# Gelu of a sum: one ScalarE pass over z itself, six equal transfers, and most adds on VectorE

## The chip, the core and the metric

The kernel runs on one core of a Trainium2 chip. The metric is device time in microseconds (us), the median over runs of the same program. One further execution is recorded by the hardware profiler, and its trace is what the views below are taken from.

The engines that appear are VectorE (DVE), ScalarE (ACT), GpSimd (POOL) and SyncE (SP), whose queue issues all transfers. The transfers themselves are carried out by 16 DMA engines.

## The reference

```
x, y: float32 [1024, 4096], random normal
z = x + y
out = 0.5 * z * (1 + tanh(sqrt(2 / pi) * (z + 0.044715 * z ** 3)))
```

This is the tanh form of gelu applied to a sum. Nothing is reduced and nothing is reused: 33.55 MB are read, 16.78 MB are written.

## The kernel before

The 1024 x 4096 tensors are viewed as 128 partitions of 32768 floats each, so every partition holds 128 KB of x, of y and of the result. One tile `z` of that size lies in SBUF. x is loaded straight into it, y is added to it in place, and the results are written over it and stored from it. y itself passes through two buffers of 8192 floats (32 KB) for each partition, used in turn.

All transfers are issued on SP, in one fixed order: the first quarter of y, the first half of x, the second quarter of y, the second half of x, the third and fourth quarters of y (lines 126 and 133), and then three stores of 16384, 10240 and 6144 floats for each partition (line 137). One row of a transfer is what one partition receives or gives, so rows of x are 64 KB, rows of y are 32 KB, and those of the stores 64, 40 and 24 KB. The first two loads are issued ahead of everything else (`begin_early`). The third and fourth loads of y wait until the adds have read the buffer that they overwrite. The first store waits, besides its data, for the first closing step of chunk 8 (`FIRST`).

The work is cut into 16 chunks of 2048 floats for each partition. A chunk goes through four steps:

- `add` (line 150): z = x + y in place, for chunks 0, 2, 4, 6, 8 and 12 on VectorE, for the other ten on GpSimd.
- `mag` (line 155): ScalarE writes |z| to a PSUM tile `w`; there are two such tiles.
- `gelu` (line 158): ScalarE applies its gelu-tanh function to -|z| in place in PSUM.
- `end` (line 167): VectorE writes max(z, 0) + w over z, which is gelu(z), since gelu(z) = max(z, 0) + gelu(-|z|).

The order on each engine is written out by hand: lists for SP, POOL, ACT and DVE are merged by a loop that takes a step when everything in `needs` is done, inside a manual schedule. The four lists and the table of needs are what fixes who waits for whom. At the end, the last wait for the last store is put behind all other closing work (`wait_late`).

Of the kernel before, what the change touches and what calls it, by code (L numbers as in the profile page):

```python
# [8 lines left out]
def begin_early(nc, count):  # L9


    head, body = (b.instructions for b in nc.main_func.blocks[:2])
    SP = mybir.EngineType.SP
    moved = [i for i in body if i.engine == SP and isinstance(i, mybir.InstDMACopy)][:count]
    assert not any(i.sync_info and i.sync_info.on_wait for i in moved)
    assert all(i.regs_accessed() == ((), ()) for i in moved)
    at = next(k for k, i in enumerate(head) if i.engine == SP)
    for k, i in enumerate(moved):
        body.remove(i)
        head.insert(at + k, i)  # L20


def wait_late(nc):

    body, end = (b.instructions for b in nc.main_func.blocks[1:3])
    last = [i for i in body if isinstance(i, mybir.InstDMACopy)][-1]
    (sem,) = [u.id for u in last.sync_info.on_update]
    all_done = end[0]  # L30
    reset = next(i for i in end if isinstance(i, mybir.InstDrain) and i.is_reset_sema)
    at = end.index(reset)
    clear = end[at + 1]
    first, stop = reset.reset_range_start, reset.reset_range_stop
    assert all_done.engine == mybir.EngineType.SP and reset.engine == mybir.EngineType.Pool
    assert isinstance(clear, mybir.InstISA) and clear.engine == mybir.EngineType.Pool
    waits = all_done.sync_info.on_wait
    (its,) = [w for w in waits if w.id == sem]

    end[0] = mybir.InstDrain(  # L40
        name=all_done.name, engine=all_done.engine, debug=all_done.debug, is_reset_sema=False,
        sync_info=mybir.SyncInfo(on_wait=[w for w in waits if w.id != sem], on_update=[]),
    )
    parts = []
    for f, e in ((first, sem), (sem + 1, stop)):
        if f < e:
            nc.gpsimd.sem_clear(range(f, e))
            parts.append(nc.cur_bb.bb.instructions.pop())
    end[at + 1 : at + 2] = parts
    end.append(  # L50
        mybir.InstEventSemaphore(
            name=clear.name, engine=mybir.EngineType.Activation, debug=clear.debug,
            sync_info=mybir.SyncInfo(
                on_wait=[its],
                on_update=[
                    mybir.SyncUpdate(
                        sync_type="semaphore", id=sem, ant_name=its.ant_name,
                        update_mode="sem-sub-imm", update_value=its.wait_value,
                    )
                ],  # L60
            ),
        )
    )


@with_exitstack
def kernel(
    ctx: ExitStack,
    tc: tile.TileContext,
    x: bass.AP,  # L70
    y: bass.AP,
    out: bass.AP,
):

    nc = tc.nc
    P = nc.NUM_PARTITIONS
    fp32 = mybir.dt.float32
    act = mybir.ActivationFunctionType
    alu = mybir.AluOpType

    N, D = x.shape
    assert N % P == 0
    TOT = N // P * D  # L90
    xv, yv, ov = (a.rearrange("(p n) d -> p (n d)", p=P) for a in (x, y, out))

    YS = 8192
    CH = 2048
    PS = 2
    xloads = [16384, 16384]
    yloads = [8192, 8192, 8192, 8192]
    FIRST = 8
    stores = [16384, 10240, 6144]

    def ranges(sizes):
        ends = [sum(sizes[: i + 1]) for i in range(len(sizes))]
        assert ends[-1] == TOT
        return [(e - f, e) for e, f in zip(ends, sizes)]

    xr, yr, sr, cr = (ranges(r) for r in (xloads, yloads, stores, [CH] * (TOT // CH)))
    C = len(cr)

    by_dve = {0: 0, 2: 0, 4: 2, 6: 4, 8: 8, 12: 10}

    def over(rs, lo, hi):
        return [i for i, (a, b) in enumerate(rs) if a < hi and b > lo]

    pool_sb = ctx.enter_context(tc.tile_pool(name="xz", bufs=1))
    pool_y = ctx.enter_context(tc.tile_pool(name="y", bufs=2))
    pool_w = ctx.enter_context(
        tc.tile_pool(name="w", bufs=PS, space=bass.MemoryType.PSUM)
    )

    one = pool_sb.tile([P, 992], fp32, tag="one", name="one")  # L120
    zt = pool_sb.tile([P, TOT], fp32, tag="z", name="z")
    yt, wt, ends = {}, {}, {}

    def load_x(i):
        a, b = xr[i]
        nc.sync.dma_start(out=zt[:, a:b], in_=xv[:, a:b])

    def load_y(i):
        a, b = yr[i]
        s, o = divmod(a, YS)  # L130
        if o == 0:
            yt[s] = pool_y.tile([P, YS], fp32, tag="y", name=f"y{s}")
        nc.sync.dma_start(out=yt[s][:, o : o + b - a], in_=yv[:, a:b])  # L133

    def store(i):
        a, b = sr[i]
        ins = nc.sync.dma_start(out=ov[:, a:b], in_=zt[:, a:b])
        if i == 0:
            tc.add_manual_dep(
                ins.ins,  # L140
                ends[FIRST].name,
                mybir.DependencyInfo(mybir.DependencyClass.Sync, mybir.DependencyReason.DATA),
                reason="the stores join the queue when the last load is nearly done",
            )

    def add(c):
        a, b = cr[c]
        s, o = divmod(a, YS)
        eng = nc.vector if c in by_dve else nc.gpsimd
        eng.tensor_add(out=zt[:, a:b], in0=zt[:, a:b], in1=yt[s][:, o : o + b - a])  # L150

    def mag(c):
        a, b = cr[c]
        wt[c] = pool_w.tile([P, CH], fp32, tag="w", name=f"w{c}")
        nc.scalar.activation(out=wt[c], in_=zt[:, a:b], func=act.Abs)  # L155

    def gelu(c):
        nc.scalar.activation(  # L158
            out=wt[c], in_=wt[c], func=act.Gelu_apprx_tanh, scale=-1.0
        )  # L160

    def end(c):
        a, b = cr[c]
        parts = 2 if c == FIRST else 1
        n = (b - a) // parts
        for o in range(0, b - a, n):
            ins = nc.vector.scalar_tensor_tensor(  # L167
                out=zt[:, a + o : a + o + n], in0=zt[:, a + o : a + o + n], scalar=0.0,
                in1=wt[c][:, o : o + n], op0=alu.max, op1=alu.add,
            )  # L170
            ends.setdefault(c, ins.ins)


    sp = [(load_y, 0), (load_x, 0), (load_y, 1), (load_x, 1), (load_y, 2), (load_y, 3)]
    sp += [(store, i) for i in range(len(stores))]
    pool = [(add, c) for c in range(C) if c not in by_dve]
    dve, acts = [], []
    for c in range(C):
        dve += [(add, k) for k in sorted(by_dve) if by_dve[k] == c] + [(end, c)]
        acts += [(mag, c), (gelu, c)]  # L180

    needs = {
        load_x: lambda i: [],
        load_y: lambda i: [
            (add, c) for c in over(cr, yr[i][0] - 2 * YS, yr[i][1] - 2 * YS)
        ],
        add: lambda c: [(load_x, i) for i in over(xr, *cr[c])]
        + [(load_y, i) for i in over(yr, *cr[c])],
        mag: lambda c: [(add, c)] + ([(end, c - PS)] if c >= PS else []),
        gelu: lambda c: [(mag, c)],  # L190
        end: lambda c: [(gelu, c)],
        store: lambda i: [(end, c) for c in over(cr, *sr[i])] + [(end, FIRST)],
    }
    queues = [sp, pool, acts, dve]
    done = set()
    with tc.manual_schedule():
        nc.vector.memset(one[:, :1], 0.0)  # L197
        nc.scalar.activation(out=one[:, :1], in_=one[:, :1], func=act.Gelu_apprx_tanh)  # L198
        while any(queues):
            moved = False  # L200
            for q in queues:
                while q and all(n in done for n in needs[q[0][0]](q[0][1])):
                    fn, arg = q.pop(0)
                    fn(arg)
                    done.add((fn, arg))
                    moved = True
                    if q is not sp:
                        break
            assert moved, [q[:1] for q in queues]

    ctx.close()
    tc.close()
    tc.compile()  # L213
    begin_early(nc, 2)
    wait_late(nc)
# [30 lines left out]
```

## Time and profile before

| quantity | value |
|---|---|
| median of 3 runs | 119.97 us (119.97 to 120.43) |
| the profiled execution: span from first to last instruction | 118.5 us |
| median less the span, what lies around it | 1.4 us |
| DVE, ACT, POOL busy | 59.8, 60.8, 55.5 us |
| bytes read, written | 33.55 MB, 16.78 MB |
| rate over the span | 425 GB/s |

How to read the views: the first part of the page gives the busy time of each engine and its share of the span. The row named DMA cuts the span into 40 equal slices and gives the mean busy share of the 16 DMA engines in tenths. The line on the queue gives its packets, its megabytes and the share of the 16 engines' span that its packets took. In the timeline a line is: start, duration, engine, line of the kernel, operation, output and inputs, shape, how many were merged, and in brackets how long the engine had been idle before and what ended that. SPq is SP's queue, and its lines named DMA_DIRECT2D are the moments at which a transfer is issued.

### The profile page before, as it was taken

To read this page: it belongs to the slowest core of one execution; us is meant where nothing else is said; L and a number is where in the kernel's file an instruction comes from. 1 tells how busy PE (TensorE), PEld (TensorE's weight loads), DVE (VectorE), ACT (ScalarE), POOL (GpSimd) and SP (SyncE) were. 2 spreads that over 40 slices of the span, in tenths; PEclk is the share of its full clock that TensorE was granted. 3 is DMA by queue.
4 is the path that set the end of the run, shared out by engine and by line. 5 is a ranking of instruction groups with operands and counts; after the bars stand their busy time and mean duration, and the time that the engine had idled before them with its cause. 6 is when DMAs were issued, how large, how long until landed. Compare 5 with 4: busy or idle time off the path is not lost.

```text
span 118.5 us, 160 instructions
## 1 busy us (share of the span) xinstructions
DVE 59.8 (50%) x24; ACT 60.8 (51%) x34; POOL 55.5 (47%) x14
## 2 busy tenths in 40 slices
DVE  0000000000399999699994594257999457742000
ACT  5000000000057989999369805797798999940000
POOL 0000000000399999998000029999999999100000
DMA  6989888998889988988899898998899889999996
GB/s 199 509 365 697 354 354 354 663 398 354 354 376 509 531 354 354 686 376 354 354 398 487 365 520 354 531 531 354 354 531 531 354 354 442 442 442 442 390 406 265
DMA packets 1296, 50.33 MB, mean 425 GB/s; under 512 B 144, under 2 KB 144, under 8 KB 144
## 3 DMA queue, kind: packets, MB, share of 16 engines
q1 hardware_dynamic: 1296, 50.33, 98.7%
HBM read 33.55 MB, written 16.78 MB: 425 GB/s over the span
## 4 chain that ended last, share of the span: by engine, by line
DMA 48%; POOL 34%; POOLq 4%; ACT 3%; DVE 2%; issue 0%; SPq 0%; DVEq 0%
POOL z L150 34%; DMA z<-in_x_dram 26%; DMA y<-in_y_dram 21%; POOLq L213 4%; DVE z L167 2%; ACT w L155 2%; ACT w L158 2%; SPq L133 0%; POOLq L150 0%; DVEq L167 0%
## 5 line engine op out<-in xcount | busy, mean ns | idle before, releaser
L150 POOL TENSOR_TENSOR z<-z,y 128x2048 f32<-128x2048 f32 x10 | 55.3, 5556 | 45.6 <-DMA z<-in_x_dram 31.1
L155 ACT ACTIVATE w<-z 128x2048 f32<-128x2048 f32 x16 | 30.1, 1880 | 42.5 <-DVE z L150 36.0
L167 DVE SCALAR_TENSOR_TENSOR z<-z,w 128x2048 f32<-128x2048 f32 (+1 forms) x17 | 36.3, 2155 | 16.0 <-ACT w L158 16.0
L150 DVE TENSOR_TENSOR z<-z,y 128x2048 f32<-128x2048 f32 x6 | 23.9, 4004 | 30.4 <-DMA z<-in_x_dram 30.1
L158 ACT ACTIVATE w<-w 128x2048 f32<-128x2048 f32 x16 | 29.8, 1862 | 0.5
L198 ACT ACT_TABLE_LOAD x1 | 1.3, 1283 | 1.3 <-PEq L230 1.3
L197 DVE MEMSET one<- 128x1 f32 x1 | 0.1, 59 | 1.3 <-PEq L230 1.3
L198 ACT ACTIVATE one<-one 128x1 f32<-128x1 f32 x1 | 0.2, 203 | 0.0
L230 POOL MEMSET const-float32-0.0<- 128x1 f32 x1 | 0.1, 100 | 0.2 <-issue 0.2
L230 POOL MEMSET const-uint8-127<- 128x1 uint8 x1 | 0.1, 103 | 0.0
L230 POOL MEMSET const-bfloat16-1.0<- 128x1 bf16 x1 | 0.1, 102 | 0.0
L230 POOL MEMSET const-float32-1.0<- 128x1 f32 x1 | 0.1, 100 | 0.0
## 6 DMA issues: line engine op xcount, KB each, us to landing
y<-in_y_dram SPq DMA_DIRECT2D x4, 4096.0 KB, 23.6
out_dram<-z SPq DMA_DIRECT2D x1, 5120.0 KB, 14.9
out_dram<-z SPq DMA_DIRECT2D x1, 3072.0 KB, 10.9
z<-in_x_dram SPq DMA_DIRECT2D x2, 44.9
out_dram<-z SPq DMA_DIRECT2D x1, 21.5
```

The lines of the kernel that those rows point to most:

```text
L150: eng.tensor_add(out=zt[:, a:b], in0=zt[:, a:b], in1=yt[s][:, o : o + b - a])
L155: nc.scalar.activation(out=wt[c], in_=zt[:, a:b], func=act.Abs)
L158: nc.scalar.activation(out=wt[c], in_=wt[c], func=act.Gelu_apprx_tanh, scale=-1.0)
L167: ins = nc.vector.scalar_tensor_tensor(out=zt[:, a + o : a + o + n], in0=zt[:, a + o : a + o + n], scalar=0.0, in1=wt[c][:, o : o + n], op ...
L197: nc.vector.memset(one[:, :1], 0.0)
L198: nc.scalar.activation(out=one[:, :1], in_=one[:, :1], func=act.Gelu_apprx_tanh)
L213: tc.compile()
L230: nc = _bacc.Bacc("TRN2", target_bir_lowering=False, num_devices=1)
```

## The change

Three things are changed together.

The computation of a chunk: `mag` and `end` are gone, and ScalarE applies gelu-tanh to z in place in SBUF, in one pass.

The transfers: there are six, all of 16384 floats for each partition, so that every row is 64 KB. y has one buffer of 64 KB for each partition; the second load of y overwrites it and waits for all eight adds of the first half. The order on SP is y, x, x, y, store, store. The extra wait of the first store is gone (`GATE = None`); each store waits for the gelus of its half.

The division of the adds: all are on VectorE but chunk 16, the last 2048 floats, which is on GpSimd. There are 17 chunks, fourteen of 2048, two of 1024 and one of 2048. For chunks 9 and 10 ScalarE copies x to PSUM first (`to_psum`), and VectorE adds y to that copy and writes z. On ScalarE the order of the second half is: the two copies, then gelu of chunks 8, 9, 10, 11, 16, 12, 13, 14, 15.

```diff
-    YS = 8192
-    CH = 2048
-    PS = 2
-    xloads = [16384, 16384]
-    yloads = [8192, 8192, 8192, 8192]
-    FIRST = 8
-    stores = [16384, 10240, 6144]
+    HALF = TOT // 2
+    xloads = [HALF, HALF]
+    yloads = [16384, 16384]
+    stores = [16384, 16384]
+    chunks = [2048] * 14 + [1024, 1024, 2048]
+    by_pool = [16]
+    in_psum = [9, 10]
+    GATE = None
...
-    by_dve = {0: 0, 2: 0, 4: 2, 6: 4, 8: 8, 12: 10}
+    second = next(c for c in range(C) if cr[c][0] == HALF)
...
+    yt = pool_y.tile([P, HALF], fp32, tag="y", name="y")
...
+    def to_psum(c):
+        a, b = cr[c]
+        xp[c] = pool_ps.tile([P, 2048], fp32, tag="xp", name=f"xp{c}")
+        nc.scalar.copy(out=xp[c][:, : b - a], in_=zt[:, a:b])
+
     def add(c):
         a, b = cr[c]
-        s, o = divmod(a, YS)
-        eng = nc.vector if c in by_dve else nc.gpsimd
-        eng.tensor_add(out=zt[:, a:b], in0=zt[:, a:b], in1=yt[s][:, o : o + b - a])
-
-    def mag(c):
+        o = a % HALF
+        eng = nc.gpsimd if c in by_pool else nc.vector
+        first = xp[c][:, : b - a] if c in in_psum else zt[:, a:b]
+        ins = eng.tensor_add(out=zt[:, a:b], in0=first, in1=yt[:, o : o + b - a])
+        adds[c] = ins.ins
+
+    def gelu(c):
         a, b = cr[c]
-        wt[c] = pool_w.tile([P, CH], fp32, tag="w", name=f"w{c}")
-        nc.scalar.activation(out=wt[c], in_=zt[:, a:b], func=act.Abs)
-
-    def gelu(c):
-        nc.scalar.activation(
-            out=wt[c], in_=wt[c], func=act.Gelu_apprx_tanh, scale=-1.0
-        )
-
-    def end(c):
...
+        nc.scalar.activation(out=zt[:, a:b], in_=zt[:, a:b], func=act.Gelu_apprx_tanh)
+
+    sp = [(load_y, i) for i in over(yr, 0, HALF)] + [(load_x, 0), (load_x, 1)]
+    sp += [(load_y, i) for i in over(yr, HALF, TOT)]
     sp += [(store, i) for i in range(len(stores))]
...
+    pool = [(add, c) for c in by_pool]
+    dve = [(add, c) for c in range(C) if c not in by_pool]
+    order = [8, 9, 10, 11, 16, 12, 13, 14, 15]
+    acts = [(gelu, c) for c in range(second)] + [(to_psum, c) for c in in_psum]
+    acts += [(gelu, c) for c in order]
...
+        load_y: lambda i: [(add, c) for c in over(cr, yr[i][0] - HALF, yr[i][1] - HALF)],
+        to_psum: lambda c: [(load_x, i) for i in over(xr, *cr[c])],
...
+        gelu: lambda c: [(add, c)],
+        store: lambda i: [(gelu, c) for c in over(cr, *sr[i])]
+        + ([(add, GATE)] if GATE is not None else []),
```

## The prediction

> **What bounds the kernel now.** I read the page first: busy shares, DMA row, queue line.
>
> ```profile
> span 118.5 us, 160 instructions
> ## 1 busy us (share of the span) xinstructions
> DVE 59.8 (50%) x24; ACT 60.8 (51%) x34; POOL 55.5 (47%) x14
> ...
> DMA  6989888998889988988899898998899889999996
> ...
> q1 hardware_dynamic: 1296, 50.33, 98.7%
> ...
> DMA 48%; POOL 34%; POOLq 4%; ACT 3%; DVE 2%; issue 0%; SPq 0%; DVEq 0%
> ```
>
> No compute engine is busy for more than half of the span, while the one DMA queue moves bytes in 98.7% of it. The chain of waits puts 34% on POOL, but only as the path back from the last store's issue; at its end the DMA was still draining earlier stores. The table by stretches shows the rate, and the timeline when transfers are issued:
>
> ```profile
> 31.40:60.40 29.00, 27.87 (x10) 22.42 (x13) 24.20 (x4) 1.00 1.00 434
> ```
> ```profile
> 44.75 0.33 SPq L133 DMA_DIRECT2D y<-in_y_dram  x1
> ...
> 57.99 0.33 SPq L133 DMA_DIRECT2D y<-in_y_dram  x1
> ...
> 77.60 0.35 SPq L137 DMA_DIRECT2D out_dram<-z  x1
> ```
>
> The columns of the first are DVE, ACT and POOL busy, clock, DMA share, GB/s: full rate. In the second, the third load of y is issued at 44.75, 15 us before the loads ahead of it land (60.4), and the first store 2.2 us before the last load lands (79.8). So the queue never empties, and compute costs nothing. The packet records of the trace (start, duration and bytes of each row) agree: the 72 rows of each of the 16 engines follow one another with no gap, from the first starts at 1.01 to 1.85 to the last ends at 117.67 to 118.13 (median 117.92); the last landing is at 118.49. Median row times are 912 ns (24 KB), 1213 (32 KB), 1514 (40 KB), 2418 (64 KB).
>
> The profiled execution is 118.5 long; the median run is 119.97, so 1.44 lies around the span. I keep that.
>
> **Part by part: the transfers themselves.** Per engine the rows before are 32 x 1.213 + 24 x 2.418 + 8 x 1.514 + 8 x 0.912 = 116.26; after, 48 x 2.418 = 116.06. Equal rows save 0.20, and fewer transfers nothing more, for queued ones have no gaps. With a queue that never empties the result is 119.77. That is also the best case; every other saving (16 Abs passes, 30.1 us of ACT; 17 closing passes, 36.4 of DVE; 9 of 10 GpSimd adds) is on engines that hide beneath the DMA already.
>
> **Where cover goes.** y has one 64 KB buffer, so the second load of y waits for all eight adds of the first half, and behind it on SP stand both stores. The second store waits for the last gelu. What covers each issue is one transfer in flight, 8 rows x 2.416 (a row less 2 to 3 ns of overlap) = 19.33.
>
> What a restart costs, "lag", is seen once: the first transfer, issued at 0, has its first rows end at 3.05 (median), 1.84 later than a row of 1.213 needs. Bounds: a queue that has run may need less; no row starts sooner than 1.01 after the issue, so 1.01 is the low end, 1.84 the high one. For the load I take 1.84, the same kind of transfer; for the store, which reads SBUF and not HBM, the middle, 1.4.
>
> [...]
>
> **First gap.** x's first half: rows end at 1.84 + 16 x 2.416 = 40.50, last landing 0.57 later (118.49 less 117.92) at 41.07. DVE begins 0.10 after the landing, as it does at 31.54 after 31.44. Its adds are then alone, without GpSimd:
>
> ```profile
> 31.54 8.79 DVE L150 TENSOR_TENSOR z<-z,y 128x2048 f32<-128x2048 f32 x2 [30.14 <-DMA z<-in_x_dram]
> 31.58 19.73 POOL L150 TENSOR_TENSOR z<-z,y 128x2048 f32<-128x2048 f32 x3 [31.14 <-DMA z<-in_x_dram]
> ...
> 40.25 4.47 DVE L167 SCALAR_TENSOR_TENSOR z<-z,w 128x2048 f32<-128x2048 f32 x2
> ...
> 44.65 2.28 DVE L150 TENSOR_TENSOR z<-z,y 128x2048 f32<-128x2048 f32 x1
> ```
>
> In the first pair DVE's first add takes 2.29, GpSimd's beside it 6.61 (its own 4.36 and DVE's before it), DVE's second 6.58: the two take turns when both read two SBUF operands. The closing passes at 40.25, one operand in PSUM, ran under a GpSimd add in 4.47 for two. So an add alone is 2.29 (2.28 at 44.65), the next 2.21 on (one starts 0.08 before the other ends). Eight: 7 x 2.21 + 2.29 = 17.76; with 0.10 ahead and 0.03 to the issue (44.72 to 44.75) y is issued at 58.96. x's second half has its rows out at 40.50 + 19.33 = 59.83. Gap 58.96 + 1.84 - 59.83 = 0.97.
>
> The gelus of the first half follow the adds; the last ends 1.9 after the last add, about 60.9, and store 0 is issued there, 19 us before y is done: free, also without the removed gate. The two copies to PSUM (2 x 1.88, the Abs row, same shape) run by 64.7, 15 us before anything needs them; if that cover went, DVE would wait at most their 3.8.
>
> **Second gap.** Times from T, y's last landing. DVE add 8 runs 0.10 to 2.39; GpSimd's add 16 waits for it and ends at 6.75 (0.14 + 6.61). Adds 9 and 10 have one operand in PSUM and run under it, to 4.60 and 6.81. Adds 11 to 13 end at 9.02, 11.23, 13.44, the half chunks (1.22, the next 1.14 on) at 14.58 and 15.72. ScalarE from SBUF to SBUF is not shown at this size. PSUM to PSUM is 1.862, SBUF to PSUM 1.880, and a 128x1 gelu in SBUF 0.203. Bounds are 1.86 and 2.07 (1.86 and the whole 0.203); I take 1.91, near the Abs row, which already reads SBUF. When one follows another without a wait, the trace starts it 0.09 before the other's end: 1.82 on. Gelus 8 to 10 keep up with the adds; gelu 11 ends at 9.05 + 1.91 = 10.96, then 16, 12, 13 at 1.82 each, 16.42, then the halves at half of 1.91, 0.96 each: 18.34. From there ACT, not DVE, is the limit. Store 1 is issued at T + 18.37. Store 0's rows end at T - 0.57 + 19.33 = T + 18.76. Gap 18.37 + 1.4 - 18.76 = 1.01. By the bounds of the gelu it is 0.3 less or 1.0 more (six passes, two of them short).
>
> [...]
>
> **Sum.** 119.77 + 0.97 + 1.01 = 121.75, or 119.77 + (lag of the load - 0.87) + (lag of the store - 0.39). At 1.01 twice it is 120.5; at 1.84 twice, 122.2; with the slowest gelus as well 123.2. A measurement of this kernel can tell about 0.5%, 0.6 us, from no change.
>
> **Rivals.**
> A quick restart, not slower: a warm queue begins within 0.9 us of the issue and its first row takes no longer than another. At 0.9 twice it is 119.77 + 0.03 + 0.51 = 120.3, no change. It decides from a sum of lags under 2.06, 1.03 each. For it: only a cold queue is shown, and store 1 before, issued 2.4 before its predecessor's rows end, showed no gap. Against: the first starts at 1.01 to 1.85. Chance 0.14.
>
> The port at the second half: adds with x in PSUM and y in SBUF also wait for GpSimd, or GpSimd gets its add in first. Add 11 and all gelus after it move by GpSimd's 4.4, so the second gap is 5.4 and the time 126.2. Against: DVE started 0.04 ahead of POOL at 31.54 and at 70.22, and passes with a PSUM operand were not held. For: there it was the second operand that lay in PSUM. Chance 0.07.
>
> The bytes move faster: over 0.5% would need 0.4 us beyond the rows' 0.20, and 64 KB rows are in the trace already at 2418 ns. Chance 0.02.
>
> **How the numbers follow.** Two gaps of about a microsecond: 0.77, 121.8. The low end 120.4 takes in the short lags and half of the quick restart, the high end 123.2 the slowest gelus with lags of 1.84; the port case and little else stay out. Faster 0.02; same is the quick restart, 0.14; slower 0.84 is the rest.
>
> **What would show it.** After, the issue of y should stand near 59.0 with x landing at 60.4, store 1's issue 18.4 after y's landing, both followed by a dip in the DMA row, and a queue share near 97%; DVE adds 2.29 throughout, gelus about 1.9. Adds 9 or 10 near 6.6 would mean the port. No dips at those issues would mean that a restart is cheap, and the forecast falls with it.

## The result, and the profile after

The changed kernel takes 124.04 us (median of 5 runs, 123.79 to 124.32) against 119.97 for the kernel before (5 runs, 119.88 to 120.6): a ratio of 1.0323, 95% interval 1.030 to 1.0347. It is slower by 3.2%. The forecast was slower by 1.5%, and 124.04 lies above the stated range.

The page of the kernel after, the same lines as shown of the one before:

```profile
span 122.5 us, 99 instructions
...
DVE 33.3 (27%) x17; ACT 35.3 (29%) x21; POOL 6.9 (6%) x5
...
DMA  9799779878977997798988998978997967797777
...
q1 hardware_dynamic: 864, 50.33, 96.8%
```

Every compute engine lost over 40% of its work (DVE 59.8 to 33.3 us, ACT 60.8 to 35.3, POOL 55.5 to 6.9) and the span grew by 4.0. The queue's share fell from 98.7% to 96.8%, and that number understates the loss: a row of 64 KB that takes more than its usual 2.42 us counts as busy all the same (0.98 at 360 GB/s from 76 to 84, below). The rate by stretches shows it better. The first fence is the kernel after, the second a variant told below (e5), in which the loss is gone; the last two columns are the DMA share and GB/s. A row counts in the stretch in which it starts, so these two are good to some per cent:

```profile
55.00:70.00 15.00, 3.92 (x2) 8.84 (x5) 0.00 (x0) 1.00 0.91 376
...
76.00:84.00 8.00, 0.33 (x1) 0.00 (x0) 0.28 (x1) 1.00 0.98 360
95.00:107.00 12.00, 4.23 (x3) 6.79 (x5) 0.00 (x0) 1.00 0.82 355
```
```profile
55.00:70.00 15.00, 4.01 (x2) 8.94 (x5) 0.00 (x0) 1.00 1.00 433
...
76.00:84.00 8.00, 7.28 (x4) 4.59 (x3) 3.92 (x1) 1.00 0.98 426
95.00:107.00 12.00, 0.00 (x0) 0.00 (x0) 0.00 (x0) 1.00 1.01 437
```

There are three places. The first and third are the two gaps that were forecast. The one in the middle, from 76 to 84, has a DMA share of 0.98 and yet only 360 GB/s. It was not forecast.

The timeline of the kernel after, with the issues on SP's queue and the start of the second half:

```profile
58.95 0.33 SPq L128 DMA_DIRECT2D y<-in_y_dram  x1
...
60.89 0.35 SPq L132 DMA_DIRECT2D out_dram<-z  x1
...
83.67 2.29 DVE L151 TENSOR_TENSOR z<-z,y 128x2048 f32<-128x2048 f32 x1 [24.74 <-DMA y<-in_y_dram]
83.72 6.65 POOL L151 TENSOR_TENSOR z<-z,y 128x2048 f32<-128x2048 f32 x1 [83.28 <-DMA y<-in_y_dram]
85.88 4.48 DVE L151 TENSOR_TENSOR z<-xp,y 128x2048 f32<-128x2048 f32 x2
...
92.59 9.20 ACT L156 ACTIVATE z<-z 128x2048 f32<-128x2048 f32 x6 [0.29 <-DVE z L151]
101.82 0.34 SPq L132 DMA_DIRECT2D out_dram<-z  x1
```

The issue of y stands at 58.95 (forecast 58.96), and store 1 is issued 18.24 after y's last landing at 83.58 (forecast 18.37). The adds from PSUM ran two in 4.48 beside GpSimd. So the forecast had the compute right. Between the issue at 58.95 and the landing at 83.58 lie 24.62 us, where the forecast had 1.84 + 19.33 + 0.57 = 21.74.

The packet records say where those 2.88 us are. "Lag" is, as in the prediction, the end of an engine's first row, less the usual time of such a row (2.418) and less the issue. The slowest engine had a lag of 3.05 (the median 2.04). Then, on all 16 engines, the eighth and last row of y took 3.18 to 4.25 us (median 3.58) and not 2.42; the 4.25 are the slowest engine's.

### The profile page after: what moved, and what is told of

Same layout as the page of the kernel before. It is cut to its first block, busy times and chain, and to the rows that moved or that the text cites. A ratio compares the mean times of both kernels' runs of the same rounds, so it can differ in the third digit from the quotient of the medians.

```text
span 122.5 us, 99 instructions
## 1 busy us (share of the span) xinstructions
DVE 33.3 (27%) x17; ACT 35.3 (29%) x21; POOL 6.9 (6%) x5
## 3 DMA queue, kind: packets, MB, share of 16 engines
q1 hardware_dynamic: 864, 50.33, 96.8%
## 4 chain that ended last, share of the span: by engine, by line
DMA 53%; DVE 20%; ACT 7%; DVEq 2%; ACTq 1%; SPq 0%; issue 0%
DMA z<-in_x_dram 33%; DMA y<-in_y_dram 20%; DVE z L151 20%; ACT z L156 7%; DVEq L198 2%; ACTq L198 1%; SPq L128 0%; DVEq L151 0%
## 5 line engine op out<-in xcount | busy, mean ns | idle before, releaser
L156 ACT ACTIVATE z<-z 128x2048 f32<-128x2048 f32 (+1 forms) x17 | 30.2, 1805 | 65.3 <-DVE z L151 65.3
L151 DVE TENSOR_TENSOR z<-z,y 128x2048 f32<-128x2048 f32 (+1 forms) x14 | 29.0, 2133 | 64.6 <-DMA z<-in_x_dram 39.8
L151 POOL TENSOR_TENSOR z<-z,y 128x2048 f32<-128x2048 f32 x1 | 6.7, 6653 | 83.3 <-DMA y<-in_y_dram 83.3
L151 DVE TENSOR_TENSOR z<-xp,y 128x2048 f32<-128x2048 f32 x2 | 4.5, 2282 | 0.0
L144 ACT COPY xp<-z 128x2048 f32<-128x2048 f32 x2 | 3.6, 1856 | 0.0
```

The lines of the kernel that those rows point to most:

```text
L144: nc.scalar.copy(out=xp[c][:, : b - a], in_=zt[:, a:b])
L151: ins = eng.tensor_add(out=zt[:, a:b], in0=first, in1=yt[:, o : o + b - a])
L156: nc.scalar.activation(out=zt[:, a:b], in_=zt[:, a:b], func=act.Gelu_apprx_tanh)
```

## The experiments

Two theories were set against each other. Theory A: the loss is the empty queue at the load of y and at store 1, and nothing else. Theory B: store 0, which is now issued 23 us before y is done (60.89 against 83.58), slows the end of the load that it stands behind. The prediction had called that issue free. Each ratio below is to the kernel before as it ran beside that variant (medians of 119.9 to 120.25).

**e1: the first gap closed.**

```diff
-    yloads = [16384, 16384]
+    yloads = [16384, 2048, 14336]
-    dve = [(add, c) for c in range(C) if c not in by_pool]
-    order = [8, 9, 10, 11, 16, 12, 13, 14, 15]
+    dve = [(add, c) for c in range(second)] + [(add, c) for c in [11, 9, 10, 8, 12, 13, 14, 15]]
+    order = [11, 9, 10, 8, 16, 12, 13, 14, 15]
```

> The second half of y is loaded in two pieces, 2048 floats (waits for add 0 alone) and 14336 (waits for all eight adds as before), and chunk 11 changes places with chunk 8 in the order of the second half so that VectorE and ScalarE still begin there only when the last piece has landed. So only the first gap is taken away. Theory A, the loss is the empty queue ahead of the load of y: the first rows of the large piece follow the small one without a gap, y lands about 79.9, and the time is 120.1 to 120.8 us. Theory B, the last row of y is slow (3.2 to 4.2 us where a row takes 2.42) because store 0 has been queued behind it early: the last rows stay slow, and the time is 121.9 to 122.6 us.

Measured: 121.39 us, 1.0104 of the kernel before (1.007 to 1.0138). y landed at 80.96, 2.6 earlier than in the changed kernel. Neither number hit: the time lies between the two, nearer to B. The last two rows of the large piece (56 KB) took 2.33 and 2.61 us at the median, against 2.12 and 2.14 of its first two, so about 0.7 stayed there. The second gap stayed too: store 1 was issued at 99.20 and its first rows began at 100.05 to 100.20, about 0.2 us after store 0's rows were out on the slowest engine (99.92) and 0.5 after the median one (99.62).

**e2: the second gap closed.** `stores = [16384, 8192, 8192]` in the changed kernel.

> The second store is cut in two of 8192 floats, the first of which waits for the gelus of chunks 8 to 11 alone; nothing else changes. Theory A, each gap costs what the slowest DMA engine loses in it: in the changed kernel that engine's last row of store 0 ended at 102.49 and the first rows of store 1 began at 102.66 to 102.81, so about 0.2 to 0.4 us are to be had, 123.6 to 123.9. Rival, a gap costs what the median engine loses in it (rows out at 100.6, next row at 102.7): 2.0 us less, about 122.0.

Measured: 124.01 us (four runs, 122.94 to 124.54), 1.0315 (1.0252 to 1.0378), no different from the changed kernel's 124.04. The rival's 2.0 us did not come; the runs spread too far to tell theory A's 0.2 to 0.4 from nothing, and the profiled one was the slowest of them, with a lag of 3.51 at the load of y on its slowest engine. The trace of the changed kernel shows why so little is to be had: the engines' lateness at the load of y is carried through store 0, whose rows are out at 100.64 on the median engine and at 102.48 on the slowest, and store 1 begins at 102.66. The median engine is idle for 2 us, the last one has hardly a pause.

**e3: nothing behind the load.** `GATE = 8` in the changed kernel, so that store 0 waits for add 8.

> Store 0 waits for add 8, so that nothing is queued behind the load of y while it runs. This makes a gap of its own at store 0: it is issued 2.4 us after y's landing T, its rows begin 1.0 later. Theory B, the store queued behind the load makes the uneven first rows and the slow last row of y: T falls from 83.6 to about 81.0, all last rows of y take 2.42, and the end is T + 2.4 + 1.0 + 38.7 + 0.4, a span of 123.5 and a time of 125.0. Theory A, the load's restart is uneven and its last row slow by itself: T stays at 83.6, the span is 126.1 and the time 127.6.

Measured: 125.6 us, 1.0461 (1.0425 to 1.0497). Its timeline:

```profile
58.90 0.33 SPq L128 DMA_DIRECT2D y<-in_y_dram  x1
...
81.47 2.29 DVE L151 TENSOR_TENSOR z<-z,y 128x2048 f32<-128x2048 f32 x1 [22.60 <-DMA y<-in_y_dram]
...
83.82 0.35 SPq L132 DMA_DIRECT2D out_dram<-z  x1
```

The same issue, but the add that waits for y starts at 81.47 and not at 83.67. The last rows of y took 2.42 to 2.56. That is theory B's mark. Its other mark, even first rows, did not come: the slowest engine still had a lag of 2.73. The total is longer because the gate makes a gap of its own at store 0, as expected.

**e4: the kernel before with an early store.** Its gate on the first store is taken out, and nothing else.

```diff
-        if i == 0:
+        if False:
...
-        store: lambda i: [(end, c) for c in over(cr, *sr[i])] + [(end, FIRST)],
+        store: lambda i: [(end, c) for c in over(cr, *sr[i])],
```

> The kernel before without the extra wait of its first store, which is then issued near 70.0 us and not at 77.6, 10 us ahead of the last load's end. Theory A, a queue that never empties does not care when the store joins it: 119.97, no change. Theory B, a store queued early slows the last rows of the load ahead of it by about 0.8 to 1.8 us: 120.8 to 121.8.

Measured: 121.08 us, 1.0085 (1.0056 to 1.0113), theory B. The store was issued at 69.84 instead of 77.60. The last two rows of y on each engine, 32 KB each, took 1.86 and 1.53 us at the median where all others took 1.21, together 0.97 too long; y landed at 80.82 and not at 79.80. No queue was empty and no compute was changed.

**e5 and e6: both gaps closed, with the store late and early.** In the changed kernel `yloads = [16384, 8192, 8192]`, and in e5 also `GATE = 10`.

> The changed kernel with the second half of y in two loads of 8192 floats (the first waits for adds 0 to 3 and is issued near 50, the second near 59) and with store 0 gated on add 10, so that it joins the queue near 76.9 us, some 2.9 ahead of y's last landing. The compute is that of the changed kernel. Theory, the whole loss is made in the queue (an empty queue at the load of y, a store queued early, an empty queue at store 1) and none of it by the one-pass compute: no gap is left, span 118.3 to 118.8, time 119.7 to 120.3, level with the kernel before. Rival, in-place gelu or the adds on VectorE cost something of their own: 121 or more.

> The same without the gate: store 0 is issued near 61, 18 us ahead of the last load's end. Theory, an early store slows the last 64 KB that each DMA engine loads by 1.0 to 1.2 us: two slow rows of 32 KB on each engine, time 120.8 to 121.2. Rival, only the distance to the last load matters or the slow rows belong to the gap: level with the gated one.

Measured: e5 120.08 us, 1.0003 (0.9989 to 1.0017), level with the kernel before. e6 121.11, 1.0093 (1.0074 to 1.0112). The timelines of e5 and then of e6:

```profile
77.05 17.34 SPq L132 DMA_DIRECT2D out_dram<-z  x2
...
79.94 11.06 DVE L151 TENSOR_TENSOR z<-z,y 128x2048 f32<-128x2048 f32 x4 [0.72 <-DMA y<-in_y_dram]
```
```profile
60.92 0.35 SPq L132 DMA_DIRECT2D out_dram<-z  x1
...
80.90 2.29 DVE L151 TENSOR_TENSOR z<-z,y 128x2048 f32<-128x2048 f32 x1 [1.70 <-DMA y<-in_y_dram]
```

The first line of each is where store 0 is issued, the second the add that waits for the last of y: 79.94 against 80.90. So in this kernel, which the queue bounds, the one-pass gelu in SBUF, the adds on VectorE and the copies cost nothing, and gain nothing either. What the change loses, it loses in the queue.

**e7: small rows at the end.** e6 with `yloads = [16384, 8192, 4096, 4096]`.

> As the last one, but the last two loads of y have 4096 floats, rows of 16 KB. If what is slowed is the last 64 KB of each engine, four rows of 16 KB are slow and the sum of the excess is again 1.0 to 1.2 us. If it is the last two rows whatever their size, two rows are slow. If the excess belongs to the row (0.3 to 0.7 each), it grows with the number of slow rows. Time 120.8 to 121.3.

Measured, one run: 120.89 us. Neither count came out. Of the last load's eight rows of 16 KB (611 ns each) for each engine, the sixth and seventh took 1044 and 809 at the median, on some engines the fifth was longer too, and the eighth was normal again at 612. So the loss is no property of a last row. It falls between 76.7 and 79.8, and begins some 48 to 64 KB ahead of the load's end on each engine.

**e8: the transfers alone.** The kernel before with the changed kernel's transfers: `YS = 16384`, one y buffer, two loads of y, two stores, order y, x, x, y.

> The transfers of the changed kernel alone on the kernel before: y in two loads of 16384 floats through one buffer, two stores, order y, x, x, y, with the adds, Abs, gelu and closing passes and the gate as before. If compute is free only while transfers cover it, the gaps now have the length of the longer compute: the load of y is issued near 67.6 (gap 9.7), store 0 about 7.4 after y's landing, store 1 about 37.4 after it; time about 149. If the transfers alone made the 3%, it would be 124.

Measured, one run: 149.22 us. The DMA row of its page:

```profile
DMA  7969696999999797008696960069696600696966
```

The zeros lie in the three stretches with an empty queue. The load of y was issued at 67.88, store 0 at 97.07, store 1 at 127.01. The faster compute of the change is what keeps these transfers at 3%.

**e9 and e10: how early is too early.** e5 with `GATE = 9` and with `GATE = 8`.

> The gated kernel with both gaps closed, store 0 gated on add 9: issued near 74.8 us instead of 77.05, so its rows could start near 75.8, before the time (76.5) from which rows were slow where the store had been queued early. Theory, a DMA engine that finds the store behind the load when it is some 64 KB from the load's end loses 0.7 to 1.2 us there: the last two rows of 32 KB are slow, 120.8 to 121.2 us. Rival, what matters is how long the store has been queued (7 us and more in the slow cases): the rows stay at 1213 ns and the time at 120.1.

> The same with store 0 gated on add 8: issued near 72.6 us. Theory: as slow as with the store issued near 61, two slow rows, 120.8 to 121.2 us. Rival: between level and slow, 120.3 to 120.8, growing with the time that the store stands queued.

Measured: e9 121.02, 1.0063 (1.0041 to 1.0084); e10 121.20, 1.0067 (1.004 to 1.0094). The store was issued at 74.81 and 72.75. The timeline of e9:

```profile
74.81 0.35 SPq L132 DMA_DIRECT2D out_dram<-z  x1
...
81.07 2.29 DVE L151 TENSOR_TENSOR z<-z,y 128x2048 f32<-128x2048 f32 x1 [1.90 <-DMA y<-in_y_dram]
```

In both the second last row took 2.24 and 2.16 us instead of 1.21. An issue at 77.05 (e5) costs nothing; one at 74.81 costs 0.6%, and one 14 us earlier (e6) 0.9%, with intervals that overlap. So the length of time that the store waits matters little. What fits all of these runs is whether the store is there when an engine comes within about 64 KB of the load's end; between 74.81 and 77.05 no run tells where the limit lies.

**e11 and e12: a load that joins an idle queue.** The load of y waits for gelu 7 too, which puts its issue 2 us later; e11 has `GATE = 8`, e12 no gate.

```diff
+        if i == 1:
+            tc.add_manual_dep(
+                ins.ins,
+                last.pop().name,
...
+        if c == second - 1:
+            last.append(ins.ins)
```

> The load of y waits for the last gelu of the first half as well, so it is issued near 60.9, when every DMA engine has been idle for 0.7 us or more; store 0 is gated on add 8, so that nothing follows the load. Theory, the restart is even (slowest engine 2.1 us from issue to the start of its effective transfer, as from a queue idle for 8 us) and becomes uneven (2.7 and more) where engines are still finishing the transfer before: first rows start within 0.7 us of one another, y lands at 82.7, time 126.8. Rival, a load restarted in mid-kernel is uneven anyhow: starts spread over 1.1 to 1.5 us, y lands at 83.3 to 83.8, time 127.4 or more.

> The same without the gate: store 0 is issued right behind the load of y, near 61.3. Theory, the early store does nothing to the first rows and slows the last row of y by 1.1 to 1.8 us: first rows start within 0.7 us, y lands at 83.8 to 84.5, time 124.3 to 125.0. Rival, the early store also makes the first rows uneven: starts spread over 1.2 us or more, slowest 3.0 and more, y lands at 84.7 or later.

Measured, one run each: 126.83 and 124.73 us. Timelines of e11 and of e12:

```profile
60.95 0.33 SPq L128 DMA_DIRECT2D y<-in_y_dram  x1
82.96 2.29 DVE L158 TENSOR_TENSOR z<-z,y 128x2048 f32<-128x2048 f32 x1 [23.97 <-DMA y<-in_y_dram]
```
```profile
61.09 0.33 SPq L128 DMA_DIRECT2D y<-in_y_dram  x1
61.47 0.42 SPq L139 DMA_DIRECT2D out_dram<-z  x1
84.35 2.29 DVE L158 TENSOR_TENSOR z<-z,y 128x2048 f32<-128x2048 f32 x1 [25.23 <-DMA y<-in_y_dram]
```

From issue to add it is 22.01 with nothing behind the load and 23.26 with the store behind it. The slow last row again: 3.61 us at the median in e12, normal in e11. The load of e12 is 2 us later than the changed kernel's, and so is its slow row, which begins at 79.7 and not at 77.5: the loss goes with the load's end and not with a moment of the run. The first rows did not start within 0.7 us of one another in either (1.3 and 1.05; one or a few engines are late), so that part of the theory missed. But the lags of the slowest engine stand apart: 2.28 and 2.21 here and 2.09 in e8, from an idle queue, against 2.73 (e3), 3.05 (the changed kernel) and 3.51 (e2) where engines were just finishing x. The early store does not decide this: e3 had none, e12 had one.

## Why the prediction was wrong

**Right.** The queue is the bound; the whole saving in compute is worth nothing (e5: 1.0003). Two gaps open, at the issues that were named. The times of the compute chain held to 0.13 us: adds 2.28 to 2.29, eight of them in 17.7 (forecast 17.76), gelus 1.91, the two copies done by 64.4. The second gap's lag was a term that was too large: stores restart in 0.93 to 0.95 us (the changed kernel, both stores of e8), where I took 1.4. That gave back 0.47 us; with the chain 0.13 shorter and the end of the last store more even by 0.14, the part behind y's landing came out 0.74 shorter than forecast. The second gap itself, forecast at 1.01, is 2.1 on the median engine but only about 0.3 on the slowest, which was late from the load of y.

**The step that failed:** "store 0 is issued there, 19 us before y is done: free, also without the removed gate" (20 us by the forecast's own times, 22.7 as measured). The prediction put this term at nothing and named no row for it: it asked only whether the store could come too late, not whether it could come too early. Its cost lies in the DMA engines, at the end of the load in front. e3 against the changed kernel, e4 against the kernel before, e6 against e5, and e12 against e11 each show it by one edit: 0.8 to 1.2 us per engine at the median, 1.83 on the slowest engine of the changed kernel. The trace of before held a hint that I didn't use. Its first store was held back to 77.6 by a gate, so that trace could show only a store that joins late; that a removed gate had no cost was not a reading of any row. The code gave the gate's reason, too: "the stores join the queue when the last load is nearly done".

**The term that was mis-sized:** the lag of the load. I priced the restart by the median engine, 1.84 (measured 2.04, and 1.75 to 1.92 in the other restarts), plus a tail of 0.57 from a queue that had run even; in that tail the slowest engine ends 0.21 after the median one, and the landing comes 0.36 later. y's landing, 83.58, came 0.41 after the last row of the slowest engine (83.17) and 2.26 after that of the median one (81.32), and the slowest engine had a lag of 3.05: 1.0 more than 1.84 and 0.21. With 1.83 for the last row and 0.05 more from that row's end to the landing, these are the 2.88 us by which y landed late; less the 0.74 they make 2.1 of the 2.2 us by which the span is over the forecast.

**The rivals.** The quick restart did not happen for loads (a lag of 3.05 where it needed about 1; over the six restarts of a load in the changed kernel, e2, e3, e8, e11 and e12 no row started sooner than 0.95 after the start of its issue); it nearly describes stores (0.93, the first row 2.45 where others take 2.42). The port did not happen: DVE was again first by 0.05 us at 83.67, and the adds with x in PSUM took 2.28 beside GpSimd. The bytes moved no faster: rows of 64 KB took 2418 ns, as before.

An early issue was right for the load of y and wrong for the store. In e5, where y was issued early in two pieces, the DMA share was 1.00 from 55 to 70 (0.91 in the changed kernel). The store of e9, issued 6.2 us ahead of y's landing, left the kernel 0.6% slower than before; that of e5, issued 2.9 ahead, left it level.

**Open.** Why a store that is ready slows the load in front of it. The store's own first rows then take the normal 2418 ns, so the time is lost and not merely shared out differently. An early issue alone does not do it. In the kernel before, the fourth load of y is issued at 57.99, 11 us before the third's rows are out, and the third's last rows take 1213 ns; in e7 store 1 is issued at 93.22, 6 us before store 0's rows are out, and these take 2418. Only a store behind a load was slow. And why some engines take up a load a microsecond late; the number of restarts is small, and which engines they were is not in the records.

## What to carry to other kernels

In the kernel before the DMA queue was busy in 98.7% of the span, and work taken off the engines gained nothing (e5: 1.0003); what counted in the change was when each transfer was issued. The load that had to wait until a whole buffer had been read left the queue empty (DMA share 0.91 from 55 to 70); cut in two, its first piece went early and covered the wait of the second (e5: 1.00). Price a restart by its slowest engine, not by the median (a lag of 3.05 against 2.04 in the changed kernel). Let a store that directly follows a load join the queue when that load is nearly done: here an issue 2.3 us before the load's rows were out cost nothing (e5), one 4.5 us before they would have been out at the usual row time cost 0.6% (e9), and earlier ones 0.7 to 0.9% (e10, e4, e6). A gate that looks like leftover caution may be what prevents it (e4: the gate alone taken out, 1.0085).

## What the runs showed that was not expected

- A store queued early behind a load lengthened the load's last 48 to 64 KB on each engine by 0.7 to 1.2 us in all at the median, with rows of 16 KB (e7), 32 KB (e4), 56 KB (e1) and 64 KB (the changed kernel, e12).
- A load restarted an idle queue with a lag of 1.75 to 1.87 us (median engine) and 2.1 to 2.3 (slowest; e8, e11, e12), and with 2.73 to 3.51 on the slowest where engines were just finishing x (e3, the changed kernel, e2); a store restarted it in 0.93 to 0.95 (median engine; the changed kernel, e8), and in the changed kernel all engines began within 0.15 us of one another.
- Engines out of step at the end of y's load (rows out at 81.32 on the median one, 83.17 on the slowest) stayed so through store 0 (100.64 and 102.48), and closing the later gap then brought little or nothing (e2: 124.01 against 124.04).
